# Query-key products of an encoder kernel: the low part's matmul over all 128 rows, with zeros under it

## The chip, the core and the metric

The kernel runs on one core of a Trainium2 chip, as a single program. The metric is device time in microseconds (us). Five engines matter here: TensorE (PE), which multiplies and loads its weights (PEld); VectorE (DVE); ScalarE (ACT); GpSimd (POOL); and SyncE (SP), which issues the transfers.

## What is computed

A bidirectional encoder of two layers, 256 tokens of width 2048, in float32. A layer is a mixer and a gated MLP. The mixer has eight heads of differential attention, four of gated linear attention and four of retention. Cut to the lines that matter for the change:

```python
# attention, per head and block of queries: two softmaxes over 64 rows of q and k each
s1 = jnp.einsum('bhqd,bhkd->bhqk', qb[..., :DIFF_QK], k1).astype(F32) * scale + bias
s2 = jnp.einsum('bhqd,bhkd->bhqk', qb[..., DIFF_QK:], k2).astype(F32) * scale + bias
p = jax.nn.softmax(s1, axis=-1) - lam * jax.nn.softmax(s2, axis=-1)
# retention, per head: 64 rows of q and k
scores = jnp.einsum('bhnid,bhnjd->bhnij', q, k) * decay[None, :, None].astype(q.dtype)
```

DIFF_QK and the retention's key width are both 64, half of TensorE's 128 rows.

## The kernel before

**The walk.** All weights lie in one array of 402 tiles ("slots"), mostly 128 x 2048. For each slot SP loads the tile (L147 to L151), ACT copies it to a float32r high part (L176), DVE subtracts to get the low part (L184), and PE multiplies (mm_feature L206 and L208, mm_token L222 to L224) with the activations, which are split in the same way. A weight slot is done on PE while ACT and DVE split the one to three slots behind it. The ring `wts` has 10 buffers.

**The tasks.** Attention heads and pairs of retention heads are generators (`diff` L629, `ret` L594). `run_tasks` (L273) is called before and after each slot's products and moves each active task by one piece, up to the next `yield`. So the order of instructions on every engine is the order in which this walk writes them, and each engine takes its own in that order.

**The products of 64 rows.** A head's queries and keys have 64 rows each, and two of them (two softmaxes, or two heads of retention) share a tile of 128 partitions. A float32 product is made from three float32r ones: hi times hi, lo times hi and hi times lo. `halves_hi_lo` (L240) lays one operand out as hi over lo, 128 rows; `halves_hi_hi` (L249) lays the other out as hi twice (tile `s`, from the ring `big` of 36 buffers of 512 columns) and keeps its low parts in a tile `l` of 256 columns (ring `sml`, 12 buffers), half m of it in the partitions 64m to 64m+63. `product` (L258) then runs two matmuls into one stretch of a bank: L263 over 128 rows gives hi.hi + lo.hi, L264 over 64 rows adds hi.lo. Each attention head and each pair of retention heads calls `product` four times, eight matmuls in a row on PE; tasks that come to this piece at the same time stand one behind the other. In `diff` three yields lie between the making of the halves and the products, so do they in `ret`. There are 16 attention heads and 4 retention pairs in both layers: 20 calls of `halves_hi_hi`, 80 of `product`.

**POOL** has little to do: a power for the factors of a norm (L318, L356), which waits on DVE's L355 or L315, and four memsets for the gated linear attention (L464, L465).

Of the kernel before, what the change touches and what calls it, by code (L numbers as in the profile page):

```python
# [14 lines left out]
AF = mybir.ActivationFunctionType  # L15
# [5 lines left out]
P = 128  # L21
# [17 lines left out]
def in_proj_order():  # L39
    """The slots of the input projection: (kind, index)."""  # L40
    s = [("gv", i) for i in range(4)]
    s += [("ga", 0), ("gq", 0), ("gk", 0), ("gq", 1), ("gk", 1)]
    s += [("rq", 0), ("rq", 1), ("rk", 0), ("rk", 1)]
    s += [("rv", i) for i in range(4)]
    for g in range(2):
        s += [("dv", 4 * g + i) for i in range(4)]
        for h in range(4 * g, 4 * g + 4):
            s += [("dq", h), ("dk", h)]
    s += [("gr", h) for h in range(4)] + [("rg", h) for h in range(4)]
    return s  # L50


def slot_list():
    """Every weight tile in the order of its use: (layer, kind, index, chunk, columns)."""
    out = []
    for l in range(DEPTH):
        for kind, i in in_proj_order():
            out.append((l, kind, i, 0, 512 if kind == "ga" else 2048))
        for o in range(KB):
            out.append((l, "wo", o, 0, 2048))  # L60
        j0 = 0
        for c, n in enumerate(CHUNKS):
            for j in range(j0, j0 + n):
                out.append((l, "upg", j, c, 2048))
                out.append((l, "upa", j, c, 2048))
            for o in range(KB):
                out.append((l, "down", o, c, n * P))
            j0 += n
    return out


# columns of the array of per-partition parameters
C_LN1, C_LN2, C_FIN, C_HG, C_GB, C_CONV = 0, 32, 64, 80, 112, 120
N_CONV = 4 * 2 * NPAIR
N_PAR = C_CONV + DEPTH * N_CONV

# columns of the array of constants
K_ID, K_COS, K_SIN, K_UP, K_UN, K_HOT = 0, 128, 384, 640, 1024, 1408
# [3 lines left out]
class Slots:  # L82
    """Tiles of one size from one tag, counted as they are taken and given back in the order of emission."""

# [15 lines left out]
def encoder_kernel(ctx: ExitStack, tc: tile.TileContext, wflat, xT, par, con, masks, gate_w, lam_p, rel_bias, decay, out):  # L100
# [43 lines left out]

# [1 line left out]
    def load(s):  # L146
# [6 lines left out]
    def parts(s):  # L153
        """The views of a tile and of its parts; those of the gates' columns lie side by side."""
        n = slots[s][4]
        if slots[s][1] == "ga":
            h = his[s][:, :1024].rearrange("p (k c) -> p k c", c=64)
            return raws[s][:, :512].rearrange("p (k c) -> p k c", c=32), h[:, :, :32], h[:, :, 32:]
        return raws[s][:, :n], his[s][:, :n], los[s][:, :n] if s in los else None

    def split_piece(s, q):
        """A quarter of a tile's split, for the first tiles."""
        if q == 0:
            his[s], los[s] = wts.get(), wts.get()
        w = slice(q * 512, (q + 1) * 512)
        act.activation(R(his[s][:, w]), raws[s][:, w], AF.Copy)  # L166
        dve.tensor_sub(R(los[s][:, w]), raws[s][:, w], his[s][:, w])  # L167
        if q == 3:
            wts.put(raws.pop(s))
# [21 lines left out]

# [1 line left out]
    middle = []  # L193

    def mm_feature(s, pt, acts, order=None):
        """Weights stationary: the first half of out[c, .] gets hi.hi, the second hi.lo + lo.hi."""
        hi, lo = his[s], los[s]
        n = len(acts)
        for k, j in enumerate(order or range(n)):
            a = acts[j]  # L200
            if k == n // 2 and middle:
                middle.pop()()
            w = slice(j * P, (j + 1) * P)
            for first in ((True, False) if k < n - 1 else (False, True)):
                if first:
                    pe.matmul(pt, lhsT=R(hi[:, w]), rhs=R(a), start=k == 0, stop=k == n - 1)  # L206
                else:
                    pe.matmul(pt[:, T:], lhsT=R(lo[:, w]), rhs=R(a[:, :T]), start=False, stop=False)  # L208
# [5 lines left out]
    def mm_token(s, pts, acts, ks):  # L214
        """Activations stationary: out[t, c] for 512 columns, the blocks ks of the contraction."""
        hi, lo = his[s], los[s]
# [9 lines left out]
    def gather(pts, m=P, rb=None, scale=None):  # L226
        """The two halves of a block's products as one, times the factor per token."""
        d, t = sml.get(), sml.get()
        act.activation(t[:m], pts[0][:m, T:], AF.Copy)  # L229
        dve.tensor_add(d[:m], t[:m], pts[0][:m, :T])  # L230
        banks.put(*pts)
        sml.put(t)
        if scale is not None:
            dve.scalar_tensor_tensor(d[:m], d[:m], scale, rb[:m], ALU.mult, ALU.mult)
        elif rb is not None:
            dve.tensor_mul(d[:m], d[:m], rb[:m])  # L236
        return d

# [1 line left out]
    def halves_hi_lo(a):  # L240
        """a's rows 0-63 and 64-127 as [hi; lo] and [lo; hi]."""
        s = big.get()
# [6 lines left out]
    def halves_hi_hi(a):  # L249
        s, l = big.get(), sml.get()  # L250
        for m in range(2):
            rows = slice(64 * m, 64 * m + 64)
            act.activation(R(s[rows, m * T:(m + 1) * T]), a[rows], AF.Copy)
            dve.tensor_sub(R(l[rows]), a[rows], s[rows, m * T:(m + 1) * T])
            act.activation(R(s[64 - 64 * m:P - 64 * m, m * T:(m + 1) * T]), a[rows], AF.Copy)
        return s, l

    def product(o, a, b, m, blk):  # L258
        """o[128, 256] = a's block blk of 128 columns against all of b, rows of half m."""
        s, l = b  # L260
        c = slice(m * T + blk * P, m * T + (blk + 1) * P)
        rows = slice(64 * m, 64 * m + 64)
        pe.matmul(o, lhsT=R(a[:, c]), rhs=R(s[:, m * T:(m + 1) * T]), start=True, stop=False)  # L263
        pe.matmul(o, lhsT=R(a[rows, c]), rhs=R(l[rows]), start=False, stop=True)  # L264

# [1 line left out]
    active, waiting = [], deque()  # L267
# [14 lines left out]

# [1 line left out]
    class Norm:  # L284
# [62 lines left out]

# [1 line left out]
    def rms_rows(n, parts):  # L349
        """Factors per token of n heads' rows of 128, parts of [P, P] in PSUM."""  # L350
        sq, m, r = sml.get(), tny.get(), tny.get()
# [8 lines left out]
    class Mixer:  # L360
# [73 lines left out]
        def transposes(self, hh):  # L434
            """A gated head's normed rows, turned, in time for its gate."""
            while hh not in self.on:
# [10 lines left out]
        def finish_pair(self, po, hh):  # L447
            """Two heads' outputs in one bank: their norm over the head's 128 values."""
            r = rms_rows(4, [po[:, i * P:(i + 1) * P] for i in range(4)])
# [144 lines left out]
        def ret(self, pr):  # L594
# [9 lines left out]
            for hp in range(2):  # L604
# [6 lines left out]
                ms.append(m)  # L611
            big.put(ks, qs[0])
            sml.put(qs[1])
            yield
# [14 lines left out]
        def diff(self, h):  # L629
# [7 lines left out]
            for m in range(2):  # L637
                for qb in range(2):
                    product(bk[m][:, qb * T:(qb + 1) * T], q, k, m, qb)
            big.put(q, k[0])  # L640
            sml.put(k[1])
            e = [big.get() for _ in range(2)]
# [66 lines left out]
    def runs(a, first, step):  # L709
        """[P, 384] seen as two runs of 256 whose starts lie 128 apart."""  # L710
        return bass.AP(a.tensor, a.offset + first, [list(a.ap[0]), [P, 2], [step, T]])

# [1 line left out]
    def decay_strips(l):  # L714
# [18 lines left out]
    def bias_strips():  # L733
        """a[r] = the bias at distance 255 - r; row p of a head's strip starts at a[p]."""
        hot, rb_t = big.get(), tny.get()
# [57 lines left out]

# [1 line left out]
    class Mlp:  # L795
# [27 lines left out]

# [1 line left out]
    outs = {}  # L825
# [17 lines left out]

# [1 line left out]
    def load_x(a, n):  # L845
# [40 lines left out]
    def evacuate(s, pts):  # L886
        """A slot's results out of PSUM; what follows the yield may wait for the next split."""
        l, kind, i, c, _ = slots[s]
# [127 lines left out]

# [1 line left out]
def lay_weights(w_in, w_o, w_up, w_down):  # L1018
# [98 lines left out]
```

## Time and profile before

| | us |
|---|---|
| median of 3 runs | 2370.15 |
| lowest and highest run | 2369.74, 2372.73 |
| span of the profiled execution | 2369.0 |

The profiled execution is known by its span, from the first to the last instruction; the median of the runs is 1.15 us more. The page shows the busy time of each engine; busy time of PE is modelled from pipelined matmuls, whose records overlap. So for PE the distance from one matmul's start to the next is read from the timeline instead.

### The profile page before, as it was taken

The page shows a single profiled execution, that of the slowest core. Times are in us where ns is not written, and L with a number is a line of the kernel's source. Part 1 is how long each engine was busy: PE and PEld are TensorE (multiplying, and loading weights), DVE is VectorE, ACT ScalarE, POOL GpSimd, SP SyncE. Part 2 cuts the span into 40 slices and gives each one's busy share as a digit, 9 for nine tenths or more (in the row PEclk, how much of TensorE's full clock was granted, in tenths as well). Part 3 has the DMA queues.
Part 4 walks back from the last instruction along what each step waited for, and adds up shares of the span by engine and source line. Part 5 has one row for each costly group of instructions (what it writes and reads, how often), then busy time and mean ns, then how long its engine had stood idle before and what let it go on. Part 6 is the DMA issues. An engine that isn't in the chain of part 4 may idle for free.

```text
span 2369.0 us, 32513 instructions
## 1 busy us (share of the span) xinstructions
PE 2351.6 (99%) x13250; PEld 2018.2 (85%) x13250; DVE 1708.7 (72%) x2459; ACT 1234.8 (52%) x1769; POOL 49.9 (2%) x37
## 2 busy tenths in 40 slices
PE   8999999999999999999999999999999999999998
PEld 7878888888888888888888888888888888888887
DVE  7977786677667765777669678767775777567764
ACT  6556664555345543555445566545553455345553
POOL 0001010000000000000000111000000000000000
PEclk9999999999999999999999999999999999999999
DMA  8443445455555555555544344455545554555552
GB/s 292 158 170 125 160 158 190 174 193 186 180 198 184 187 187 191 183 189 181 193 180 169 125 160 143 176 183 179 195 165 198 190 192 176 189 192 193 178 183 102
DMA packets 66644, 423.09 MB, mean 179 GB/s; under 512 B 7960, under 2 KB 10904, under 8 KB 28096
## 3 DMA queue, kind: packets, MB, share of 16 engines
q1 hardware_dynamic: 66352, 420.96, 50.6%
q8 instruction: 104, 1.70, 0.3%
q14 instruction: 44, 0.36, 0.0%
q10 hardware_dynamic: 144, 0.06, 0.0%
HBM read 417.83 MB, written 2.11 MB: 177 GB/s over the span
## 4 chain that ended last, share of the span: by engine, by line
PE 98%; DVE 2%; DMA 0%; ACT 0%; issue 0%; ACTq 0%; SPq 0%; DVEq 0%
PE bank L206 57%; PE bank L208 29%; PE bank L222 2%; PE bank L223 2%; PE bank L224 2%; PE bank L264 1%; PE bank L263 1%; PE bank L683 1%; DVE wts L184 0%; PE bank L541 0%; PE bank L212 0%; PE bank L622 0%; DVE big L526 0%; PE bank L672 0%; DVE big L566 0%; DMA wts<-wflat 0%
## 5 line engine op out<-in xcount | busy, mean ns | idle before, releaser
L206 PE MATMUL bank<-big,wts 128*128 128x512 f32 x5760 | 2020.3, 399 | 0.0
L208 PE MATMUL bank<-big,wts 128*128 128x256 f32 x5760 | 1557.9, 281 | 0.0
L206 PEld LDWEIGHTS bank<-big,wts 128*128 128x128 f32 x5760 | 1062.8, 188 | 232.9 <-issue 0.9
L208 PEld LDWEIGHTS bank<-big,wts 128*128 128x128 f32 x5760 | 1089.1, 189 | 32.6
L176 ACT ACTIVATE wts<-wts 128x2048 fp32r<-128x2048 f32 (+3 forms) x398 | 744.2, 1872 | 366.9 <-PE bank L208 349.4
L184 DVE TENSOR_TENSOR wts<-wts,wts 128x2048 fp32r<-128x2048 f32 (+3 forms) x398 | 888.4, 2233 | 11.2 <-PE bank L223 7.5
L894 DVE TENSOR_TENSOR x<-bank,x 128x256 f32<-128x256 f32 x256 | 108.7, 425 | 244.8 <-PE bank L206 240.4
L230 DVE TENSOR_TENSOR sml<-sml,bank 128x256 f32<-128x256 f32 (+1 forms) x242 | 101.7, 420 | 227.7 <-ACT sml L229 227.5
L229 ACT ACTIVATE sml<-bank 128x256 f32<-128x256 f32 (+1 forms) x242 | 92.2, 381 | 190.6 <-PE bank L206 190.4
L819 ACT ACTIVATE big<-sml 128x256 fp32r<-128x256 f32 x88 | 36.8, 418 | 190.6 <-DVE sml L817 190.6
L814 ACT ACTIVATE sml<-sml 128x256 f32<-128x256 f32 x88 | 36.8, 418 | 158.9 <-DVE sml L807 158.9
L222 PE MATMUL bank<-wts,big 128*128 128x512 f32 x256 | 103.8, 406 | 6.0 <-ACT wts L166 6.0
L805 ACT ACTIVATE sml<-sml,conv_t 128x256 f32<-128x256 f32 x176 | 103.7, 589 | 5.7 <-DVE sml L236 5.7
L236 DVE TENSOR_TENSOR sml<-sml,sml 128x256 f32<-128x256 f32 (+1 forms) x230 | 97.7, 425 | 7.9
L223 PE MATMUL bank<-wts,big 128*128 128x512 f32 x256 | 101.4, 396 | 0.0
L224 PE MATMUL bank<-wts,big 128*128 128x512 f32 x256 | 101.3, 396 | 0.0
L806 DVE SCALAR_TENSOR_TENSOR sml<-sml,conv_t,sml 128x255 f32<-128x255 f32 x176 | 84.2, 479 | 8.7 <-ACT sml L805 8.7
L807 DVE SCALAR_TENSOR_TENSOR sml<-sml,conv_t,sml 128x255 f32<-128x255 f32 x176 | 85.2, 484 | 6.3
L820 DVE TENSOR_TENSOR big<-sml,big 128x256 fp32r<-128x256 f32 x88 | 37.4, 425 | 42.6 <-ACT big L819 42.6
L222 PEld LDWEIGHTS bank<-wts,big 128*128 128x128 f32 x256 | 49.0, 191 | 18.0 <-ACT wts L166 6.0
L224 PEld LDWEIGHTS bank<-wts,big 128*128 128x128 f32 x256 | 48.9, 191 | 10.5
L223 PEld LDWEIGHTS bank<-wts,big 128*128 128x128 f32 x256 | 48.9, 191 | 10.1 <-DVE wts L167 0.4
(146 smaller groups left out, 1027.7 us busy)
## 6 DMA issues: line engine op xcount, KB each, us to landing
wts<-wflat SPq DMA_DIRECT2D x300, 1024.0 KB, 4.8
wts<-wflat SPq DMA_DIRECT2D x64, 960.0 KB, 4.7
wts<-wflat SPq DMA_DIRECT2D x32, 896.0 KB, 4.6
wts<-wflat SPq DMA_DIRECT2D x18, 256.0 KB, 5.8
x<-xT SPq DMA_DIRECT2D x8, 256.0 KB, 5.9
out<-big SPq DMA_DIRECT2D x8, 256.0 KB, 3.8
strips<-dr SPq DMA_DIRECT2D x1, 1536.0 KB, 8.6
sml<-sml SPq DMA_DIRECT2D x32, 32.0 KB, 2.1
```

The lines of the kernel that those rows point to most:

```text
L176: act.activation(R(hi), raw, AF.Copy)
L184: dve.tensor_sub(R(lo), raw, hi)
L206: pe.matmul(pt, lhsT=R(hi[:, w]), rhs=R(a), start=k == 0, stop=k == n - 1)
L208: pe.matmul(pt[:, T:], lhsT=R(lo[:, w]), rhs=R(a[:, :T]), start=False, stop=False)
L222: pe.matmul(pts[tb], lhsT=al, rhs=R(hi[:, w]), start=k == 0, stop=False)
L223: pe.matmul(pts[tb], lhsT=ah, rhs=R(lo[:, w]), start=False, stop=False)
L224: pe.matmul(pts[tb], lhsT=ah, rhs=R(hi[:, w]), start=False, stop=k == KB - 1)
L229: act.activation(t[:m], pts[0][:m, T:], AF.Copy)
L230: dve.tensor_add(d[:m], t[:m], pts[0][:m, :T])
L236: dve.tensor_mul(d[:m], d[:m], rb[:m])
L805: act.activation(c, us, AF.Identity, scale=w[1], bias=w[3])
L894: dve.tensor_add(xb[i], pts[0][:, h * T:(h + 1) * T], xb[i])
```

## The change

`halves_hi_hi` takes the tile `l` from the ring `big` (512 columns). For each half m it writes the low part to the columns of half m, in the partitions of half m, and lets POOL set the other 64 partitions of those columns to zero. `product` multiplies all 128 rows of the second operand with the same weights as the first matmul: hi.lo from the half that holds the low part, zero from the other. ACT's and DVE's instructions keep their number and shape. `ret` and `diff` give `l` back to `big`. The rest of the diff takes out comments and docstrings.

```diff
     def halves_hi_hi(a):
-        s, l = big.get(), sml.get()
+
+        s, l = big.get(), big.get()
         for m in range(2):
-            rows = slice(64 * m, 64 * m + 64)
-            act.activation(R(s[rows, m * T:(m + 1) * T]), a[rows], AF.Copy)
-            dve.tensor_sub(R(l[rows]), a[rows], s[rows, m * T:(m + 1) * T])
-            act.activation(R(s[64 - 64 * m:P - 64 * m, m * T:(m + 1) * T]), a[rows], AF.Copy)
+            rows, other, w = slice(64 * m, 64 * m + 64), slice(64 - 64 * m, P - 64 * m), slice(m * T, (m + 1) * T)
+            pool.memset(l[other, w], 0.0)
+            act.activation(R(s[rows, w]), a[rows], AF.Copy)
+            dve.tensor_sub(R(l[rows, w]), a[rows], s[rows, w])
+            act.activation(R(s[other, w]), a[rows], AF.Copy)
         return s, l
...
     def product(o, a, b, m, blk):
...
         c = slice(m * T + blk * P, m * T + (blk + 1) * P)
-        rows = slice(64 * m, 64 * m + 64)
-        pe.matmul(o, lhsT=R(a[:, c]), rhs=R(s[:, m * T:(m + 1) * T]), start=True, stop=False)
-        pe.matmul(o, lhsT=R(a[rows, c]), rhs=R(l[rows]), start=False, stop=True)
+        w = slice(m * T, (m + 1) * T)
+        pe.matmul(o, lhsT=R(a[:, c]), rhs=R(s[:, w]), start=True, stop=False)
+        pe.matmul(o, lhsT=R(a[:, c]), rhs=R(l[:, w]), start=False, stop=True)
...
-            big.put(ks, qs[0])
-            sml.put(qs[1])
+            big.put(ks, *qs)
...
-            big.put(q, k[0])
-            sml.put(k[1])
+            big.put(q, *k)
```

## Rows read from the trace of the kernel before

**Rows 1.** The page, busy us (share of the span) xinstructions.

```profile
PE 2351.6 (99%) x13250; PEld 2018.2 (85%) x13250; DVE 1708.7 (72%) x2459; ACT 1234.8 (52%) x1769; POOL 49.9 (2%) x37
```

**Rows 2.** The page, chain of work that ended last, by engine.

```profile
PE 98%; DVE 2%; DMA 0%; ACT 0%; issue 0%; ACTq 0%; SPq 0%; DVEq 0%
```

**Rows 3.** Groups of PE by line and shape: busy us, mean ns.

```profile
L264 PE MATMUL bank<-sml,big 64*128 64x256 f32 x80 | 31.1, 389 | 0.0
L263 PE MATMUL bank<-big,big 128*128 128x256 f32 x80 | 30.8, 385 | 0.0
```

**Rows 4.** Timeline of PE, first group of products: start us, us, instruction.

```profile
164.90 0.40 PE L208 MATMUL bank<-big,wts 128*128 128x256 f32 x2
165.14 0.40 PE L206 MATMUL bank<-big,wts 128*128 128x512 f32 x1
165.38 0.28 PE L263 MATMUL bank<-big,big 128*128 128x256 f32 x1
165.59 0.38 PE L264 MATMUL bank<-sml,big 64*128 64x256 f32 x1
165.90 0.38 PE L263 MATMUL bank<-big,big 128*128 128x256 f32 x1
...
174.02 0.79 PE L206 MATMUL bank<-big,wts 128*128 128x512 f32 x1
```

**Rows 5.** Timeline of PEld, weight loads at the same place.

```profile
164.90 0.19 PEld L208 LDWEIGHTS bank<-big,wts 128*128 128x128 f32 x1
...
165.59 0.18 PEld L264 LDWEIGHTS bank<-sml,big 64*128 64x128 f32 x1 [0.26 <-DVE sml L236]
```

**Rows 6.** Timeline of PE, a group of eight, and one of sixteen.

```profile
261.14 0.36 PE L263 MATMUL bank<-big,big 128*128 128x256 f32 x1
...
263.62 0.50 PE L206 MATMUL bank<-big,wts 128*128 128x512 f32 x1
263.96 0.28 PE L208 MATMUL bank<-big,wts 128*128 128x256 f32 x1
...
203.02 0.28 PE L263 MATMUL bank<-big,big 128*128 128x256 f32 x1
...
207.93 0.50 PE L222 MATMUL bank<-wts,big 128*128 128x512 f32 x1
```

**Rows 7.** Timeline of PE, weights' products behind a transpose (L443).

```profile
293.11 0.48 PE L206 MATMUL bank<-big,wts 128*128 128x512 f32 x1
293.42 0.28 PE L208 MATMUL bank<-big,wts 128*128 128x256 f32 x1
```

**Rows 8.** Stretches: length, busy PE, PEld, DVE, ACT, POOL; clock, DMA share, GB/s.

```profile
170.80:177.50 6.70, 6.70 (x18) 4.71 (x18) 4.99 (x6) 3.02 (x9) 0.00 (x0) 0.50 0.00 1
208.40:211.60 3.20, 3.20 (x9) 2.48 (x8) 3.17 (x4) 2.87 (x9) 0.00 (x0) 0.50 0.00 0
1348.40:1351.70 3.30, 3.30 (x13) 2.82 (x12) 3.23 (x5) 3.13 (x9) 0.00 (x0) 0.50 0.01 2
...
140.00:346.00 206.00, 206.00 (x1121) 171.80 (x1120) 158.51 (x270) 126.29 (x271) 21.17 (x12) 0.98 0.42 146
```

**Rows 9.** POOL's memset group and a power; DVE's L324 with memsets and without.

```profile
L464 POOL MEMSET big<- 128x512 f32 x2 | 1.1, 526 | 0.0
...
200.02 2.67 POOL L356 TENSOR_TENSOR tny<-tny,mhalf 128x2 f32<-128x2 f32 x1 [9.98 <-DVE tny L355]
...
41.38 1.05 DVE L324 TENSOR_SCALAR sml<-ident,tny 128x128 f32<-128x128 f32 x2 [0.82 <-POOL tny L318]
...
444.55 0.48 DVE L324 TENSOR_SCALAR sml<-ident,tny 128x128 f32<-128x128 f32 x2 [0.87 <-POOL tny L318]
```

**Rows 10.** DVE ahead of the first group: last low part, a split; its slot on PE.

```profile
163.94 0.42 DVE L254 TENSOR_TENSOR sml<-sml,big 64x256 fp32r<-64x256 f32 x1 [0.45 <-ACT big L253]
...
152.82 2.28 DVE L184 TENSOR_TENSOR wts<-wts,wts 128x2048 fp32r<-128x2048 f32 x1
...
159.72 0.39 PE L206 MATMUL bank<-big,wts 128*128 128x512 f32 x1
```

## The prediction

> **What bounds the kernel now.** I read the page's busy times first: PE 99%, DVE 72%, ACT 52%, POOL 2% [rows 1]. PE's busy time is modelled, so the second look is the chain of waits: 98% of it is PE [rows 2]. The kernel ends when PE has gone through its matmuls, and an instruction there costs the distance from its start to the next start. The third view, the groups by line and shape, counts the instructions that the change touches: 80 matmuls of L263 over 128 rows and 80 of L264 over 64 rows [rows 3]. Their mean durations say little, since records overlap; so the fourth view is the timeline of PE around the first of them.
>
> There the reader is to see two rhythms. Two weights' products of 128x256 (L208) take 0.24 us together, from 164.90 to 165.14: 0.12 each; one of 128x512 (L206) takes 0.24. From 165.59 to 165.90 a product of the same 256 columns takes 0.31 [rows 4]. The loads tell why. L208's second load starts at 164.90, when the matmul ahead of it starts, and is hidden under it; L264's load starts only at 165.59, 0.21 after the matmul ahead of it, and its own matmul starts with it [rows 4, 5]. So where the row count changes between 128 and 64, the load of 0.19 us [rows 5] is not hidden. The 160 matmuls alternate, so nearly all of them pay.
>
> **What the change removes.** The products stand in 16 groups. One has 24 matmuls (three tasks) and takes 8.64 us, from 165.38 to 174.02 [rows 4]. Two have 16; the one shown takes 4.91, from 203.02 to 207.93, the other, in layer 1, is alike. Thirteen have eight; the one shown takes 2.48, from 261.14 to 263.62 [rows 6]. Sum: 8.64 + 2 x 4.91 + 13 x 2.48 = 50.7 us for 160 matmuls.
>
> After the change all are 128x128 weights against 128x256, the shape of L208. I take 0.12 each: 160 x 0.12 = 19.2 us. No row shows eight of that shape in a row, so the bounds are wide: 0.31, if each keeps its unhidden load, and, since nothing in the rows excludes a little less than 0.12, some 0.11 below. L208 is the nearest row by shape, rows and type, so I take its value.
>
> Two edges go with it. Thirteen groups are entered from transposes or other small matmuls. A weights' matmul entered so takes 0.31 instead of 0.24, from 293.11 to 293.42 [rows 7]; this 0.07 to 0.08 stays, 13 x 0.08 = 1.0 us. At the way out, the weights' matmul behind a group takes 0.34 instead of 0.24, from 263.62 to 263.96 [rows 6]; that 0.10 goes. Four groups are followed by a transpose, where I count nothing, and three by the slow stretches below, where it is counted: 9 x 0.10 = 0.9 us. So far 50.7 - 19.2 - 1.0 + 0.9 = 31.4 us, all of it on the chain.
>
> **The clock.** The granted clock is 0.50 (1.2 GHz) in three stretches: 170.8 to 177.5, 208.4 to 211.6 and 1348.4 to 1351.7 [rows 8]. Each begins at the end of, or right behind, one of the three long groups; no group of eight has one. Before each fall the engine ran the alternating products alone. After the change these products come in the rhythm of the weights' products, during which the clock is 2.4 GHz for hundreds of us, so I expect no fall. The part inside the first group, up to 174.02, is in its 8.64 already. Outside lie 177.5 - 174.02 = 3.5, 3.2 and 3.3 us: 10.0 us of work that takes half at full clock, 5.0 us saved. The ends are 0 (all three falls stay) and 5.0; I take 5.0.
>
> **What it adds.** 40 memsets of 64x256 on POOL. L464's 128x512 takes 0.53 [rows 9]; with half the columns each takes 0.26 to 0.53, 10 to 21 us on an engine that is 2% busy. They need no data, only a free buffer and POOL's turn, and the products come three yields later. The thinnest cover: the last low part before the first group (L254) ends at 163.94 + 0.42 = 164.36 [rows 10], the group starts at 165.38 [rows 4], so DVE has 1.0 us in hand, and the memset, issued with it but waiting for no ACT or DVE result, has more. On PE I cost it at nothing.
>
> On DVE it can cost something. Two L324 take 1.05 us beside two memsets and 0.48 without [rows 9], 0.29 per memset; 40 of them are 12 us of DVE at most, zero at least. In layer 0's mixer, 140 to 346, DVE is busy for 158.5 of 206 us [rows 8]. That layer has 80 of the 160 matmuls (half of 31.4) and two of the slow stretches (3.4 us), some 19 us of what PE saves, which leaves 158.5 + 6 of 187 us, 88%. And the splits run ahead: the one at 152.82 ends at 155.10, PE uses it at 159.72 [rows 10], 4.6 us later, in the densest part. So I take zero; if that cover were gone, up to 12 us would come back. The Trainium skill, page "SBUF — State Buffer", section "Who interferes with whom", has DVE's subtraction of two SBUF inputs contend with GpSimd's reads but not with a GpSimd instruction that only writes; by it the price beside L184 is zero, and no row here shows a memset beside L184.
>
> The tile `l` comes from a ring of 36 instead of 12; ACT and DVE do the same instructions on it. No transfer and no queue of SP is added. PE frees weight buffers earlier, so loads come earlier; the transfers' share is 0.42 in that stretch [rows 8]. What is late next is DVE's split, at 88%, not yet PE's bound.
>
> **Sum.** 31.4 + 5.0 = 36.4 us. The profiled span is 2369.0, the median of the runs 2370.15, 1.15 above; the terms are differences, so I take them from the median: 2370.15 - 36.4 = 2333.7 us.
>
> **The rivals.**
> **The clock still falls.** The matmuls get faster, the three stretches stay: 2338.7. For it: each fall stands at such a place. Against it: after the change PE has no unhidden load there. 10%.
> **The load stays unhidden.** The distance of 0.31 is load 0.19 plus matmul 0.12; if not the change of rows but something else of these products keeps the load back, 160 x 0.31 + 1.0 is what they cost today: 2370. Against it: the weights' products, all of 128 rows, hide theirs, L208 at 164.90 for one [rows 4, 5]. The Trainium skill, page "TensorE: Matmul & The Clock Gate", "Part 3: Packing small matmuls — row/col tiling", lets a weight load overlap with running matmuls only where the row groups differ; by that rule two 128-row matmuls in a row would never overlap and the change would bring nothing, and the row of L208 says otherwise. 3%.
> **DVE becomes the bound in the mixer.** Memsets and the shorter stage use up the splits' lead, PE waits on L184: all 12 us come back, 2345.7. Against it the 88% and the lead. 6%.
> **Slower: POOL's queue.** POOL takes its instructions in order, and its power L356 waits for statistics from DVE and can itself take 2.67 us beside a split [rows 9]. If a group's memsets stood behind it and the group came right after, PE would wait up to 2.67 + 2 x 0.53 = 3.7 us, with weights' products of later slots queued behind. It decides from 36.4 / 16 = 2.3 us per group; at 3.7 in all 16, 59.7 us, the time is 2393. Against it: memsets are issued with the halves, three yields before the products. 3%.
>
> **How the numbers follow.** The forecast has 78%, the rivals 10, 3, 6 and 3. Below, 0.11 per matmul gives 1.6 us more, and the entry edge may go: 2330. Above, 2338.7 with still fallen clocks plus a third of DVE's 12 us: 2343. That leaves out half of DVE's case, the unhidden load, POOL's queue and a tenth for what I haven't seen, under 2 in 10. About 0.2% (4.7 us) is what a measurement of this kernel can tell from no change. Faster by more: 0.94; within: 0.03; slower: 0.03.
>
> **What the profile after would show.** Right: the second matmul of `product` with 128 rows, both lines at 0.12 from start to start, a group of eight in about 1.0 us and the first group in 2.9; clock 1.00 after the long groups. Wrong: distances of 0.31 there; stretches at 0.50; PE or its loads waiting on POOL at the product's lines, or on L184 in the mixers; longer L184 beside memsets.

## The result, and the profile after

The changed kernel takes 2334.18 us (median; 2333.44 to 2334.36) against 2369.99 before (now the median of four runs): a ratio of 0.9848, 95% interval 0.9834 to 0.9862, 35.8 us less. The spans of the two profiled executions are 2369.0 and 2332.3, 36.7 apart. The forecast was 2333.7.

The page of the changed kernel, busy times and the chain by engine, beside [rows 1, 2]:

```profile
PE 2315.1 (99%) x13250; PEld 2004.0 (86%) x13250; DVE 1704.8 (73%) x2459; ACT 1231.6 (53%) x1769; POOL 62.3 (3%) x77
...
PE 98%; DVE 2%; DMA 0%; ACT 0%; issue 0%; ACTq 0%; SPq 0%; DVEq 0%
```

PE is the bound as before, with as many matmuls: the kernel does the same number of instructions on PE, DVE and ACT, and 40 more on POOL. What fell is the distance between matmuls. The groups by line and shape, where L265 and L266 are the two matmuls of `product` and L254 the memset (for [rows 3]):

```profile
L265 PE MATMUL bank<-big,big 128*128 128x256 f32 x80 | 20.8, 296 | 0.0
L266 PE MATMUL bank<-big,big 128*128 128x256 f32 x80 | 19.8, 282 | 0.0
...
L254 POOL MEMSET big<- 64x256 f32 x40 | 12.2, 306 | 75.9 <-DVE big L550 59.7 <-PE bank L266 14.2
```

Both have 128 rows now. The timeline of PE at the first group and its end, and one weight load there (for [rows 4, 5]):

```profile
165.66 0.28 PE L265 MATMUL bank<-big,big 128*128 128x256 f32 x1
165.78 0.28 PE L266 MATMUL bank<-big,big 128*128 128x256 f32 x1
165.90 0.28 PE L265 MATMUL bank<-big,big 128*128 128x256 f32 x1
...
168.52 0.40 PE L206 MATMUL bank<-big,wts 128*128 128x512 f32 x1
...
165.66 0.19 PEld L266 LDWEIGHTS bank<-big,big 128*128 128x128 f32 x1
```

The reader sees 0.12 us from start to start where it was 0.31, and L266's load starting at 165.66, with the matmul ahead of it, where L264's started 0.21 us after it. The group of 24 takes 168.52 - 165.66 = 2.86 us for 8.64. A group of eight, its entrance from two transposes and its way out (for [rows 6, 7]):

```profile
247.62 0.38 PE L700 MATMUL bank<-ident,sml 128*128 128x128 f32 x2
247.75 0.36 PE L265 MATMUL bank<-big,big 128*128 128x256 f32 x1
247.95 0.28 PE L266 MATMUL bank<-big,big 128*128 128x256 f32 x1
...
248.79 0.40 PE L206 MATMUL bank<-big,wts 128*128 128x512 f32 x1
249.02 0.28 PE L208 MATMUL bank<-big,wts 128*128 128x256 f32 x1
```

248.79 - 247.75 = 1.04 us for 2.48; behind it L206 is followed at 0.23 where it was 0.34. All 16 groups together, added up from the timeline in the same way, take 20.15 us for 50.7.

Stretches at the places of [rows 8]: behind the first group, and layer 0's mixer, which now ends some 19 us earlier (columns as there):

```profile
168.60:178.00 9.40, 9.40 (x67) 8.61 (x66) 9.19 (x17) 5.08 (x16) 0.00 (x0) 1.00 0.40 150
140.00:326.70 186.70, 186.70 (x1126) 164.25 (x1125) 156.47 (x270) 124.83 (x271) 27.36 (x32) 1.00 0.45 162
```

The granted clock is 1.00 (2.4 GHz) where it was 0.50, and nowhere between the first products and the last few us of the execution is there a lower stretch. DVE does the same 270 instructions there as before and is busy for 156.5 of 186.7 us, 84%. The waits of PE, all of them (us in total, times, longest):

```profile
PE bank L222 <- ACT wts L166: 6.0, 1, 6.0
PE bank L314 <- ACT sml L295: 1.4, 1, 1.4
PE bank L543 <- DVE big L561: 0.2, 1, 0.2
```

They are those of before (6.0, 1.4 and 0.2 us); no wait on POOL or on a split (L184) has come.

### The profile page after: what moved, and what is told of

The parts are those of the page before. It is cut to its first block, busy times and chain, and to the rows that moved or that the text cites. A ratio compares the mean times of both kernels' runs of the same rounds, so it can differ in the third digit from the quotient of the medians.

```text
span 2332.3 us, 32603 instructions
## 1 busy us (share of the span) xinstructions
PE 2315.1 (99%) x13250; PEld 2004.0 (86%) x13250; DVE 1704.8 (73%) x2459; ACT 1231.6 (53%) x1769; POOL 62.3 (3%) x77
## 4 chain that ended last, share of the span: by engine, by line
PE 98%; DVE 2%; DMA 0%; ACT 0%; issue 0%; ACTq 0%; SPq 0%; DVEq 0%
PE bank L206 58%; PE bank L208 29%; PE bank L222 2%; PE bank L223 2%; PE bank L224 2%; PE bank L683 1%; DVE wts L184 0%; PE bank L543 0%; PE bank L265 0%; PE bank L266 0%; DVE big L528 0%; PE bank L212 0%; PE bank L623 0%; PE bank L672 0%; DVE big L568 0%; DMA wts<-wflat 0%
## 5 line engine op out<-in xcount | busy, mean ns | idle before, releaser
L206 PE MATMUL bank<-big,wts 128*128 128x512 f32 x5760 | 2016.8, 398 | 0.0
L208 PE MATMUL bank<-big,wts 128*128 128x256 f32 x5760 | 1556.6, 281 | 0.0
L206 PEld LDWEIGHTS bank<-big,wts 128*128 128x128 f32 x5760 | 1061.4, 188 | 231.6 <-PE bank L591 0.9
L208 PEld LDWEIGHTS bank<-big,wts 128*128 128x128 f32 x5760 | 1087.4, 189 | 32.6
L184 DVE TENSOR_TENSOR wts<-wts,wts 128x2048 fp32r<-128x2048 f32 (+3 forms) x398 | 888.4, 2233 | 12.3 <-PE bank L223 8.2
```

Source lines behind the costliest of these rows:

```text
L184: dve.tensor_sub(R(lo), raw, hi)
```

## The experiments

**64 rows again, all else kept.** This kernel separates PE's row count from the tile's move and the memsets.

```diff
-    def product(o, a, b, m, blk):
...
+    def product(o, a, b, m, blk, narrow=False):
...
+        rows = slice(64 * m, 64 * m + 64) if narrow else slice(0, P)
...
-        pe.matmul(o, lhsT=R(a[:, c]), rhs=R(l[:, w]), start=False, stop=True)
+        pe.matmul(o, lhsT=R(a[rows, c]), rhs=R(l[rows, w]), start=False, stop=True)
...
-                    product(bk[m][:, qb * T:(qb + 1) * T], q, k, m, qb)
+                    product(bk[m][:, qb * T:(qb + 1) * T], q, k, m, qb, True)
```

The call in `ret` asks for it in the same way.

> The changed kernel with its memsets and its tile of 512 columns, but the second matmul of product over 64 rows again. Theory (the whole gain is the change of row count on PE): groups of eight at 2.48 us from the first product to the next weights' matmul, three stretches at a clock of 0.50, 2370 us, the time before the change. Rival (the moved tile or anything else of the change gives a part of the gain): under 2367. Second rival (memsets and tile cost something that the gain covered): over 2372.

Measured: 2369.37 us, a ratio of 0.9994 to the kernel before, 0.9985 to 1.0004: no gain is left, and the memsets and the larger tile cost nothing that shows. The 16 groups take 50.6 us, groups of eight 2.48. The three stretches at half clock that the theory asked for did not all come: its profile has two of them, the third place stayed at full clock:

```profile
171.30:178.00 6.70, 6.70 (x17) 4.80 (x18) 5.05 (x7) 3.24 (x9) 0.00 (x0) 0.50 0.00 1
208.80:212.10 3.30, 3.30 (x9) 2.59 (x8) 3.27 (x3) 3.07 (x9) 0.00 (x0) 0.50 0.00 0
1347.80:1352.00 4.20, 4.20 (x25) 3.64 (x24) 4.09 (x7) 3.69 (x9) 0.00 (x0) 1.00 0.02 6
```

What that third stretch, 3.3 us long in the kernel before, costs can be read from the two timelines, from the end of the long group to the first product of the next group. The first two lines are of the kernel before, the others of this one:

```profile
1347.57 0.50 PE L206 MATMUL bank<-big,wts 128*128 128x512 f32 x1
1362.49 0.36 PE L263 MATMUL bank<-big,big 128*128 128x256 f32 x1
...
1347.78 0.51 PE L206 MATMUL bank<-big,wts 128*128 128x512 f32 x1
1361.22 0.36 PE L265 MATMUL bank<-big,big 128*128 128x256 f32 x1
```

14.92 us against 13.44: 1.5 us; the two spans differ by 2369.0 - 2367.4 = 1.6. So the falls don't come in every execution. The scatter of the kernel before (2368.8 to 2373.2 in this series of 13 runs) goes with it: its four runs above 2372 us have a mean granted clock of 0.994, the nine others, up to 2371.0, one of 0.995 or 0.996.

**Half the changes of row count.** The same 160 matmuls, 80 of them over 64 rows, but of two products in a row the second takes its 64-row matmul first.

```diff
-        pe.matmul(o, lhsT=R(a[:, c]), rhs=R(s[:, w]), start=True, stop=False)
-        pe.matmul(o, lhsT=R(a[:, c]), rhs=R(l[:, w]), start=False, stop=True)
+        rows = slice(64 * m, 64 * m + 64)
+        if not second:
+            pe.matmul(o, lhsT=R(a[:, c]), rhs=R(s[:, w]), start=True, stop=False)
+        pe.matmul(o, lhsT=R(a[rows, c]), rhs=R(l[rows, w]), start=second, stop=not second)
+        if second:
+            pe.matmul(o, lhsT=R(a[:, c]), rhs=R(s[:, w]), start=False, stop=True)
```

> As the run before, but of two products in a row the second takes its 64-row matmul first: 128, 64, 64, 128 rows. Each group of eight has 4 changes of row count for 8, and as many 64-row matmuls. Theory (each change costs 0.19 us, worked out from (2.48 + 0.10 - 1.04) / 8): 64 behind 64 at 0.12, a group of eight about 1.8 us, 2334.2 + 80 x 0.19 = 2349.4 us, and up to 5 more where the clock falls behind the long groups. Rival (a 64-row matmul is slow whatever stands before it, or a load never overlaps in the same rows): 64 behind 64 at 0.31 as well, 120 slow distances, 2334.2 + 120 x 0.19 = 2357 us, and up to 5 more.

Measured: 2348.99 us (2348.62 to 2349.34), a group of eight 1.81 us. The sum is the theory's: (1.81 - 1.04) / 4 = 0.19 us per change, as (2.48 + 0.10 - 1.04) / 8 = 0.19 is with eight. But the rows are not as I expected them. PE and PEld at the first group (L266 and L269 have 128 rows, L267 64):

```profile
166.05 0.28 PE L266 MATMUL bank<-big,big 128*128 128x256 f32 x1
166.26 0.50 PE L267 MATMUL bank<-big,big 64*128 64x256 f32 x2
166.69 0.39 PE L269 MATMUL bank<-big,big 128*128 128x256 f32 x1
166.92 0.28 PE L266 MATMUL bank<-big,big 128*128 128x256 f32 x1
...
166.26 0.29 PEld L267 LDWEIGHTS bank<-big,big 64*128 64x128 f32 x2 [0.26 <-DVE sml L236]
...
166.80 0.19 PEld L266 LDWEIGHTS bank<-big,big 128*128 128x128 f32 x1
```

The two matmuls of L267 start at 166.26 and 166.26 + 0.50 - 0.28 = 166.48. So all distances are near 0.22: 0.21 where the row count changes, 0.22 or 0.23 behind a matmul that has changed it. The two 64-row loads start within 0.11 us of each other, so a load of the same rows does run ahead, over 64 rows as over 128. What a change costs has two parts, then: about 0.09 because the load behind it starts only 0.21 after the matmul ahead has started, and 0.10 behind that, read as its own matmul waiting for it: the matmul's record starts with its load and is 0.39 long (L269) where one without a change has 0.28 (L266), and the next matmul starts that much later. Where every matmul changes, both fall on each: 0.12 + 0.09 + 0.10 = 0.31.

**The same number of changes, in the long groups and in the short.** 56 of the 160 matmuls are made alternating again: once in the seven tasks of the three long groups, once in seven tasks that stand alone in groups of eight.

```diff
-                    product(bk[m][:, qb * T:(qb + 1) * T], q, k, m, qb)
+                    product(bk[m][:, qb * T:(qb + 1) * T], q, k, m, qb, (l, h) in ((0, 0), (0, 1), (0, 2), (1, 0)))
```

The last argument asks for 64 rows; in `ret` it does so for (0, 0), (0, 1) and (1, 1) in the first kernel. The second has (0, 3), (0, 4), (0, 5), (1, 1), (1, 2), (1, 3) and (1, 4) in `diff` and none in `ret`.

> The changed kernel with 64 rows again in the seven tasks whose products stand in the three long groups (56 matmuls): 56 changes of row count come back, 56 x 0.19 = 10.8 us. Theory (the clock falls because of these groups): three stretches at 0.50 come back too, 4.7 to 5.0 us: 2334.2 + 10.8 + 4.8 = 2349.8 us. Rival (the falls have nothing to do with the groups): no stretch at 0.50, 2345.0.

> The changed kernel with 64 rows again in seven tasks whose products stand alone in groups of eight (56 matmuls): the same 56 changes, 10.8 us. Theory: clock 1.00 all through, 2334.2 + 10.8 = 2345.0 us, some 5 us less than with the same number of changes in the long groups. Rival (the falls are not bound to the long groups): the clock falls here as well, 2348 to 2350.

Measured: 2350.79 us (2350.18 to 2352.82) with the long groups, 2345.02 (2344.67 to 2345.36) with the short, 5.8 us apart for the same changes. Stretches of the first kernel behind its long groups:

```profile
169.60:179.70 10.10, 10.10 (x26) 7.31 (x27) 7.65 (x13) 3.99 (x9) 0.00 (x0) 0.50 0.00 1
207.20:213.90 6.70, 6.70 (x15) 4.58 (x16) 5.93 (x9) 5.32 (x17) 0.00 (x0) 0.50 0.02 9
1340.40:1343.70 3.30, 3.30 (x11) 2.69 (x11) 3.27 (x4) 2.72 (x9) 0.00 (x0) 0.50 0.01 2
```

and of the second at two of its alternating groups of eight:

```profile
216.90:222.00 5.10, 5.10 (x22) 3.62 (x21) 4.12 (x7) 3.05 (x15) 1.39 (x2) 1.00 0.46 191
1341.40:1347.00 5.60, 5.60 (x28) 4.15 (x27) 5.01 (x11) 2.38 (x9) 1.06 (x3) 1.00 0.54 187
```

The clock falls behind the long alternating groups and not behind the short. The granted clock of every run agrees: its mean is 0.994 to 0.996 in the four runs with the long groups and 0.998 in all four with the short, as in all four of the changed kernel. The clock's part is a term of its own, of about the size that the prediction gave it (5.0), and it varies: 20.1 us at half clock here, 13.2 in [rows 8], 10.0 in the first experiment. The profiled execution here is the longest of its four, 2 us over the median.

**The memsets, five times and not at all.** Three kernels on one chip: the changed kernel again, one that writes each memset five times, and one whose low parts go to three tiles of their own, set to zero once.

```diff
-            pool.memset(l[other, w], 0.0)
+            for _ in range(5):
+                pool.memset(l[other, w], 0.0)
```

```diff
+    zeros = [st.tile([P, 2 * T], F32, name=f"zl{i}") for i in range(3)]
...
+    for z in zeros:
+        pool.memset(z, 0.0)
...
-        s, l = big.get(), big.get()
+        s, l = big.get(), zeros[taken[0] % 3]
+        taken[0] += 1
...
-            pool.memset(l[other, w], 0.0)
```

> The changed kernel again, beside the next two on the same chip: 2334 us, by both theories; the two below are read against it.

> The changed kernel with each memset written five times: 200 memsets, 61 us of POOL for 12. Theory (memsets hide, POOL runs ahead of PE, and DVE has room): within 2 us of the changed kernel, no wait of PE on POOL. Rival (memsets take DVE's time and the splits lose their lead): 160 more memsets, up to 0.29 us of DVE each, 46 us of DVE and PE waits on the splits in the mixers, 2340 to 2380 us. Second rival (POOL's queue): PE waits on the memsets or DVE on the powers behind them, a few us.

> The changed kernel without the 40 memsets: the low parts go to three tiles of their own that are set to zero once at the start (ring big 34 buffers, sml 10). Theory: the memsets cost nothing, so this is within 2 us of the changed kernel. Rival (memsets cost DVE or PE some us): faster by 2 to 12 us. Second rival (three tiles or smaller rings make DVE wait for a tile's last reader): slower.

Measured: 2333.85 us (2333.15 to 2335.05), 2334.31 (2333.48 to 2334.61) and 2334.44 (2333.89 to 2334.66). The three can't be told apart. POOL's groups of the kernel with five, and of the one with none:

```profile
L255 POOL MEMSET big<- 64x256 f32 x200 | 61.3, 307 | 73.5 <-DVE big L551 59.7 <-PE bank L267 2.5
```

```profile
L243 POOL MEMSET zl<- 128x512 f32 x3 | 1.4, 525 | 0.3 <-POOLq L1115 0.3
```

With 61 us of memsets for 12, PE's list of waits is the same three lines and DVE's busy time 1704.6 us for 1704.8. So 40 memsets are costed rightly at nothing, and leaving them out has nothing to give.

## Why the prediction was right

**The products.** 160 matmuls at 0.12 were to take 19.2 us and 1.0 at the entrances, 20.2; they take 20.15. The row of L208 was the right one to take the distance from, although no row showed more than two such matmuls together.

**The edges.** The way out gives back its 0.10, as worked out. The 0.08 at the entrances stays in the sum on both sides, but it isn't a cost of the group: the second transpose is recorded 0.03 before the first product, which is followed at 0.20, and the two make 0.23, a transpose (0.11) and a product (0.12). The record puts the product's start about 0.08 early, and the long distance behind it holds work of the transpose ahead. Behind the thirteen groups other than the long ones the two traces differ by 1.3 us in all, where 0.9 was worked out: the four followed by a transpose, counted at nothing, give back some 0.1 each too.

**The clock.** Predicted 5.0 us. From the end of a long group to the first product of the next group, the kernel before takes 29.00, 20.93 and 14.92 us, the changed one 27.41, 19.20 and 13.45: 4.8 us, the ways out of these three groups (0.1 each) included, as in the 5.0. One step of that term was wrong in size: work at half clock does not take twice its time here. A pair of weights' products behind the first group, in the kernel before:

```profile
174.83 0.63 PE L206 MATMUL bank<-big,wts 128*128 128x512 f32 x1
175.26 0.41 PE L208 MATMUL bank<-big,wts 128*128 128x256 f32 x1
175.47 0.63 PE L206 MATMUL bank<-big,wts 128*128 128x512 f32 x1
```

It takes 0.64 us where [rows 4] have 0.24 + 0.12 = 0.36 at full clock, 1.8 times as long, so the 10.0 us at half clock are worth 4.4, and the ways out bring it near the 4.8. Nor did the alternating products run alone right up to each fall: some 0.5 and 0.8 us of weights' products lie between the second and the third long group and the stretches behind them (207.93 to 208.4, 1347.57 to 1348.4). The whole is then 30.6 for the groups (50.7 - 20.15), 4.8 and 1.3: 36.7, the difference of the two spans. The forecast's 36.4 has two small misses of opposite sign in it, 0.2 too much for the clock and 0.4 too little for the ways out; that they nearly cancel is luck.

**Why there is a slow distance at all.** Here my words were too simple, though the terms held: I read 0.31 as a load of 0.19 that isn't hidden plus a matmul of 0.12. The kernel with pairs shows that 0.19 is the price of a change of row count, in two parts; why it equals the recorded duration of the load is not shown. It is paid per change, not per 64-row matmul: with 80 changes and just as many narrow matmuls the groups' time is about halfway, 35.6 us between 20.15 and 50.6. The Trainium skill, page "TensorEngine Tiling (Array Packing)", section "Tiling Modes", lists 64 rows as a mode of its own and says that changing the mode, not just the tile, drains TensorE. The 0.19 us per change agrees, and so does the load that starts only 0.21 us after the matmul ahead.

**The rivals.** The unhidden load fell: loads of the same rows start with the matmul ahead. The rule of the Trainium skill that went with it (page "TensorE: Matmul & The Clock Gate", "Part 3: Packing small matmuls — row/col tiling", overlap only where row groups differ) doesn't hold in these runs, over 128 rows nor over 64; the same Part names loads into a background weight buffer as another case, and by that the overlap is allowed. DVE as the bound fell: 84% in layer 0's mixer where 88% was worked out, and its subtraction takes no more time beside a memset. POOL and DVE of the changed kernel:

```profile
152.08 2.11 POOL L254 MEMSET big<- 64x256 f32 x6
...
153.10 2.28 DVE L184 TENSOR_TENSOR wts<-wts,wts 128x2048 fp32r<-128x2048 f32 x1
```

Six memsets, of 0.31 each, run from 152.08 to 154.19, the second half of that beside L184, which takes its 2.28. The price of 0.29 per memset, taken from L324 [rows 9], is not paid here. The Trainium skill's "SBUF — State Buffer", section "Who interferes with whom", had it so, and the trace agrees. POOL's queue as a cause of waits fell too: those six end at 154.19, and the first group starts at 165.66. The clock's staying low behind the long groups didn't come.

## What to carry to other kernels

Cost a matmul by the distance to the next start, and look for places where the row count alternates: here each change cost 0.19 us, more than a matmul of 256 columns, and 64 rows of zeros in their place cost PE nothing that shows. Where rows can't be filled, order the matmuls so that the count changes less often; half the changes cost half in the groups. And look for what a long stretch of alternating matmuls does behind its end: some 5.7 of the 36.7 us were the clock that no longer fell, 4.5 behind the long groups (the 4.8 less the ways out) and 1.2 inside the first (8.64 for 24 x 0.31).

## What had not been expected

Distances of 0.22 between two 64-row matmuls, as told, and the clock's loose tie to the groups. In the kernel with pairs the group of 24 takes 5.17 us and the clock stays at 1.00 behind it; its mean granted clock is 0.998 in all four runs:

```profile
166.00:178.00 12.00, 12.00 (x68) 9.53 (x68) 11.75 (x19) 5.78 (x12) 0.00 (x0) 1.00 0.28 94
```

while it fell behind a group of 16 alternating matmuls that takes 4.91 [rows 6, 8], and not behind the same group in layer 1 of the first experiment. So a long group of alternating matmuls brings the fall, but not every one in every execution, and its length in time alone isn't what decides. Nor is it the zeros that keep the clock up: the kernel with pairs multiplies none of them. What decides stays open. The groups of 64-row matmuls of the gated linear attention still change the row count on their way in and out; nothing was tried there.
